# A held-over retention, a fourth raw buffer and longer paces in a hybrid attention/retention step

## The chip, the cores and the metric

The kernel runs on one core of a Trainium2 chip. The metric is the device time of one execution in microseconds (us), taken as the median of several executions. A profile is one more execution, recorded by the hardware; it has a time of its own.

The engines are named as in the profile: PE does the matmuls (PEld loads the stationary operand), DVE and ACT do elementwise work, POOL does masks and issues some DMAs, SP issues most DMAs. An engine works through its instructions in order. An instruction whose input isn't there yet holds up whatever stands behind it on the same engine or DMA queue.

## The reference

One step of a one-layer encoder over a prompt of 1024 frames and 8 running streams of 16 frames (128 sample frames), model width 2048, all in float32:

```
h = rms_norm(x, norm_pre);  p = h @ w_in            # 2048 x 8192
q_sb,k_sb,v_sb,gate_sb, q_r,k_r,v_r,gate_r = split(p)   # 8 heads of 128 each
stick-breaking: z = q k^T / sqrt(128); a = exp(log_sigmoid(z) + sum of later log_sigmoid(-z)), strictly causal; o = a v
retention (rotary q, k; chunks of 64): o = (q k^T * decay) v + decay_read * q S;  S = gamma^n S + k^T (decay_write v)
y = concat(head_rms_norm(o) * silu(gate));  out = y @ w_out;  x = x + rms_norm(out, norm_post)
```

The sample frames use a cache of 1024 past keys and values and a retention state per stream. The new keys, values and states are outputs too.

## The kernel before

**Tiles and groups.** Tokens come in tiles of 128 rows. Group 0 (`gi` 0) is prompt tiles 0 to 3 and the sample tile, group 1 (`gi` 1) is prompt tiles 4 to 7. For each group a loop runs over 8 heads, and for each head over "panels" of projection matmuls: `rows` (values and gates, 192 matmuls in group 1, L467), `ret_keys` and `ret_queries` (48 matmuls each, L410), `attention` (48 for the queries and 48 for the keys). A product of two float32 operands is made of three matmuls, so each weight block is split into a high and a low half by ACT and DVE (L173, L174). The order of the panels is rows, ret_keys, ret_queries, attention; in the last head of group 1 it is rows, attention, ret_keys, ret_last.

**Jobs and ticks.** All other work is in generators, called jobs: `ret_branch` (retention of one head, L1068 on), `sb_branch` (stick-breaking attention, L1094 on, with `stick_breaking` L781), `decode` (sample attention over the cache), and loads and splits for the output projection. A job yields a number of ticks; the panels call `tick()` after each product matmul (0.75 tick each in `rows`), and a tick runs at most one step of a job that is due. So a "pace" such as `D_RET` is a count of product matmuls to be put between two steps. `drain(job)` calls `tick()` until a job is done, with no matmul of a panel between: whatever is due in those ticks, of any job, is written out back to back.

**The planner.** The written order is a priority and not the final order. Tile's planner lays out each engine's order by simulating the engines: it takes the first instruction in the written order whose inputs are there by its own costs. Once laid out, the order is fixed, and on the chip an engine waits where the costs were too low.

**Around the changed places.** A head's retention builds `rk` and `rq` with rotary (`rope`, L507), writes `rk` to memory and reads it back in pieces to transpose it (`turn_out` L692, `turn_in` L701, DVE L797/L772/L1083), then does four blocks: scores (L957), output (L975, L982), state (L992, L997), one `D_RET` between output and state and another before the next block. `finish` normalises, gates, turns the output around through memory and stores it in `s_y`. In `sb_branch` each tile has matmuls z (L807), sigmoids, a scan (L737), a product (L738), a turn through memory (POOL L692, L701), a transpose (L797) and the product with the values (L834). `D_TB` stands between z and the rest, `D_TR` ahead of the last two products with the values. For group 0 the attention output is transposed into `kT`, a tile with one buffer.

For head 0 of group 1, `ret_keys` drains the retention of head 7 of group 0 ahead of its own `rope`. `attention` then drains the attention and the decode jobs of that head too and swaps the buffers `ip` and `psd` for `ip2` and `psx`.

The output projection is seven products of quarter matrices. In the last head, `first_left` (L1127) prepares the left operand of the first: `left` (L333) loads four pairs of blocks in three raw buffers `mr` (the fourth load waits until the first pair is split) and splits them. Its steps are taken between the weight blocks of the panel `ret_last`. Then come the products (5,0), (5,1), (1,0), (3,0), (3,1), under which the last retention and attention run: 72, 72, 72, 48 and 48 matmuls, one tick per matmul.

Of the kernel before, what the change touches and what calls it, by code (L numbers as in the profile page):

```python
# [18 lines left out]
P = 128  # L19
D = 2048  # L20
KT = D // P
H = 8
# [44 lines left out]
MR = 3  # L67
# [26 lines left out]
def tile_hybrid_step(  # L94
# [238 lines left out]
    def left(gi, n, hi, lo, bufs, tag, deep, wait):  # L333
        src = LEFT[n]
        raw = []

        def load(pair):
            r = bufs.tile([P, 2, 256], F32, name=tag, tag=tag, bufs=deep)
            if src[0] == "y":
                rows = s_y[gi][src[1] * H // 2 + pair][:, :, src[2] * 256 : src[2] * 256 + 256]  # L340
            else:
                rows = s_s[gi][pair][:, :, src[1], :]
            pin(nc.sync.dma_start(r, rows))
            raw.extend((r[:, 0], r[:, 1]))

        for pair in range(deep):
            load(pair)
        yield wait
        for h in range(HT):
            pin(*split(hi[h], lo[h], raw.pop(0)))  # L350
            if h % 2 and h // 2 + deep < HT // 2:
                load(h // 2 + deep)
            yield D_OP
# [127 lines left out]
    with ExitStack() as s1:  # L481
# [299 lines left out]
        def stick_breaking(g, h, out, q2, k2, rest):  # L781
# [3 lines left out]
            for step in range(len(todo) + lag):  # L785
# [33 lines left out]
                if step < len(todo):  # L819
                    if early:  # L820
                        yield D_TB[phase[0]]
# [3 lines left out]
                if step >= lag:  # L825
# [4 lines left out]
                    if step >= len(todo) and (early or step > len(todo)):  # L830
                        yield D_TR[phase[0]] + overlap()
# [10 lines left out]
        waiting = []  # L842

# [108 lines left out]

        def retention(gi, g, h, out, rq, rk, rkn, rv, dT, natural):
# [14 lines left out]
            for i in range(4):  # L968
# [3 lines left out]
                elif SAMPLE in g["tiles"]:  # L972
                    nxt = scores(4, 1)
                po = acc_tile()
# [15 lines left out]
                yield D_RET[phase[0]]  # L990
# [11 lines left out]
                yield D_RET[phase[0]]  # L1002
# [4 lines left out]
        def sample_retention(h, out, sc, rq, rkn, rv):  # L1007
# [26 lines left out]
            if not read:  # L1034
                waiting.clear()
                read_states()
            po = read[0]
# [55 lines left out]

        def sb_branch(gi, g, h, out, q2, k2, kT, rest):  # L1094
# [18 lines left out]
        summed, sampled, lefts, mine = [], [], [], {}  # L1113

# [12 lines left out]
        def first_left():  # L1127
# [3 lines left out]
            return left(0, 5, *mine[0, 5], wp, "mr", MR, D_LEFT)  # L1131
# [3 lines left out]
        for gi, g in enumerate(GROUPS):  # L1135
# [6 lines left out]
            for h in range(H):  # L1142
# [11 lines left out]
                def ret_queries(acc=None):  # L1154
                    rows_in["rq"] = rope(acc or project(g, mov, col(4, h)), "rq", *ropes)

                def ret_keys(acc=None):
# [4 lines left out]
                    acc = acc or project(g, mov, col(5, h))  # L1162
                    drain(ret_job)
                    ret_job = Job(ret_branch(gi, g, h, rows_in, rope(acc, "rk", *ropes)), D_NAT[phase[0]])
# [13 lines left out]
                def attention():  # L1178
# [9 lines left out]
                    if gi == 1 and h == 0:  # L1188
                        drain(sub)
                        late.close()  # L1190
# [473 lines left out]
```

## Time and profile before

| | |
|---|---|
| time, median of 3 runs | 2242.17 us (2240.48 to 2243.14) |
| the profiled execution | 2244.6 us, span of its instructions 2242.4 us |
| PE busy / share of the span | 2218.3 us / 99% |
| DVE, ACT, POOL busy | 1264.3, 919.3, 430.5 us |
| mean DMA rate | 209 GB/s |
| granted TensorE clock | 0.999 |

PE is busy for nearly the whole span, so a change can only take away idle time of PE, or add to it. The records of matmuls overlap, since a matmul's end is modelled: two starts of a full product are closer together than one record is long, and a stall shows as idle time only beyond that overlap. In the timelines a row gives start, duration, engine, line, operation, tiles, shape and count; in brackets at its end stand the idle time of the engine ahead of it and what ended it.

### The profile page before, as it was taken

What the parts mean: (1) busy time and instruction counts of PE and PEld (TensorE: products, weight loads), DVE (VectorE), ACT (ScalarE), POOL (GpSimd) and SP (SyncE); (2) the same over time, 40 slices, a digit from 0 to 9 for tenths busy, and PEclk for the clock granted to TensorE, in tenths of its full rate; (3) what the DMA queues carried; (4) which work ended last, traced back from release to release, by engine and by line L of the source; (5) the groups of instructions that cost most, each with busy time, mean ns of one, the idle gap of its engine ahead of it and who ended that gap; (6) DMA issues with size and microseconds to landing.
All of it is one profiled execution on the core that took longest, in us unless ns stands there. A gap on an engine that the chain in (4) does not pass through costs nothing. (4 is left out here: it accounts for less than half of the span.)

```text
span 2242.4 us, 34745 instructions
## 1 busy us (share of the span) xinstructions
PE 2218.3 (99%) x12046; PEld 1886.3 (84%) x12046; DVE 1264.3 (56%) x2690; ACT 919.3 (41%) x1999; POOL 430.5 (19%) x723
## 2 busy tenths in 40 slices
PE   9999999999999999999999999999999999999998
PEld 8888889798888979888788888888888887778887
DVE  5435445453454545356666665756666657556577
ACT  7423333333333333334433443443434445545463
POOL 1022131222213132221222112120202212000020
PEclk9999999999999999999999999999999999999999
DMA  8567575566757656677868777878788777865785
GB/s 294 178 197 204 172 198 174 176 190 209 193 173 196 183 171 194 202 202 269 233 182 239 220 227 232 235 228 235 221 233 230 211 224 188 235 220 161 220 224 170
DMA packets 379297, 467.83 MB, mean 209 GB/s; under 512 B 118128, under 2 KB 235632, under 8 KB 378608
## 3 DMA queue, kind: packets, MB, share of 16 engines
q1 hardware_dynamic: 250608, 290.58, 43.8%
q0 software_dynamic: 36432, 95.72, 15.8%
q10 hardware_dynamic: 92080, 79.32, 11.2%
q8 instruction: 94, 1.54, 0.3%
q14 instruction: 83, 0.68, 0.1%
HBM read 364.56 MB, written 106.95 MB: 210 GB/s over the span
## 5 line engine op out<-in xcount | busy, mean ns | idle before, releaser
L467 PE MATMUL accm<-whn,mh 128*128 128x512 f32 x1152 | 452.1, 393 | 0.5 <-DVE rq L513 0.5
L467 PE MATMUL accm<-whn,ml 128*128 128x512 f32 x1152 | 452.3, 393 | 0.0
L467 PE MATMUL accm<-wln,mh 128*128 128x512 f32 x1152 | 451.3, 392 | 0.0
L410 PE MATMUL acc<-ml,wh 128*128 128x256 f32 (+2 forms) x1536 | 445.8, 341 | 0.6 <-DVE ml L180 0.3
L173 ACT ACTIVATE wh<-wr 128x512 fp32r<-128x512 f32 x408 | 255.9, 631 | 459.6 <-PE acc L410 190.0
L410 PE MATMUL acc<-mh,wl 128*128 128x256 f32 (+2 forms) x1536 | 444.1, 340 | 0.0
L410 PE MATMUL acc<-mh,wh 128*128 128x256 f32 (+2 forms) x1536 | 442.2, 339 | 0.5 <-ACT mh L179 0.4
L174 DVE TENSOR_TENSOR wl<-wr,wh 128x512 fp32r<-128x512 f32 x408 | 279.4, 688 | 261.5 <-ACT wh L173 241.7
L174 DVE TENSOR_TENSOR wln<-wrn,whn 128x512 fp32r<-128x512 f32 x256 | 175.9, 689 | 285.7 <-ACT whn L173 282.8
L173 ACT ACTIVATE whn<-wrn 128x512 fp32r<-128x512 f32 x256 | 161.4, 631 | 391.7 <-PE accm L467 259.3
L410 PEld LDWEIGHTS acc<-mh,wl 128*128 128x128 f32 x1536 | 281.2, 188 | 23.8 <-issue 5.4
L410 PEld LDWEIGHTS acc<-mh,wh 128*128 128x128 f32 x1536 | 283.0, 188 | 20.3 <-ACT mh L179 0.9
L410 PEld LDWEIGHTS acc<-ml,wh 128*128 128x128 f32 x1536 | 280.3, 188 | 20.9 <-DVE ml L180 1.6
L467 PEld LDWEIGHTS accm<-whn,mh 128*128 128x128 f32 x1152 | 216.5, 188 | 44.6 <-DVE rq L513 0.9
L467 PEld LDWEIGHTS accm<-whn,ml 128*128 128x128 f32 x1152 | 216.5, 188 | 43.4 <-issue 0.8
L467 PEld LDWEIGHTS accm<-wln,mh 128*128 128x128 f32 x1152 | 216.5, 188 | 43.1
L701 POOL DMA_DIRECT2D be<-s_be x128 | 94.2, 742 | 159.2 <-DMA s_be<-be 132.3
L737 DVE TENSOR_TENSOR_SCAN kp<-kp 128x1152 f32<-128x1152 f32 (+4 forms) x40 | 82.7, 2069 | 56.1 <-POOL kp L726 28.3
L1262 PE MATMUL a<-wh,mh 128*128 128x512 f32 x240 | 94.6, 394 | 0.1
L1265 PE MATMUL a<-wl,mh 128*128 128x512 f32 x240 | 93.9, 391 | 0.3 <-DVE wl L174 0.3
L1266 PE MATMUL a<-wh,ml 128*128 128x512 f32 x240 | 93.5, 390 | 0.0
L726 POOL TENSOR_SCALAR_AFFINE_SELECT kp<-kp 128x128 f32<-128x128 f32 x40 | 13.6, 341 | 362.9 <-ACT kp L720 362.8
(287 smaller groups left out, 3011.9 us busy)
## 6 DMA issues: line engine op xcount, KB each, us to landing
wrn<-w_rows SPq DMA_DIRECT2D x256, 256.0 KB, 3.7
wr<-w_cols SPq DMA_DIRECT2D x255, 256.0 KB, 4.4
kcT<-cache_k POOLq DMA_DIRECT2D x64, 512.0 KB, 4.7
vc<-cache_v SPq DMA_DIRECT2D x64, 512.0 KB, 5.2
wr<-s_b SPq DMA_DIRECT2D x80, 256.0 KB, 3.7
wr<-w_out SPq DMA_DIRECT2D x80, 256.0 KB, 4.1
br<-w_out SPq DMA_DIRECT2D x64, 256.0 KB, 4.6
s_b<-br ACTq DMA_DIRECT2D x32, 512.0 KB, 4.6
```

The source lines that it names most:

```text
L173: nc.scalar.activation(hi, src, AF.Copy),
L174: nc.vector.tensor_tensor(lo, src, hi.bitcast(F32), ALU.subtract),
L410: last = nc.tensor.matmul(a[:, :m], lhs[:, j, :], rhs[w][:, j, o : o + m], start=(w == 0 and j == 0 and n == 0), stop=(w == KT // WQ - 1 a ...
L467: anchor[0] = nc.tensor.matmul(banks[t], lhs[q][:, j, ts], rhs, start=(k == 0 and n == 0), stop=(k == KT - 1 and n == 2),)
L701: q.dma_start(raw[32 * i : 32 * i + 32, :].rearrange("p (k a) -> p k a", a=32), s[:, :, 32 * i : 32 * i + 32].rearrange("k (j b) a -> b (k ...
L726: nc.gpsimd.affine_select(blk, blk, pattern=[[-1, P]], base=0, channel_multiplier=1, compare_op=ALU.is_gt, fill=fill,)
L737: nc.vector.tensor_tensor_scan(rev, rev, rev, 1.0, ALU.mult, ALU.bypass)
L1262: ins = nc.tensor.matmul(a, hi[k][:, ts], wh, start=first, stop=False)
L1265: nc.tensor.matmul(a, hi[k][:, ts], wl, start=False, stop=False)
L1266: anchor[0] = nc.tensor.matmul(a, lo[k][:, ts], wh, start=False, stop=last)
```

## The change

- **Retention held over.** In head 0 of group 1, `ret_keys` no longer drains the retention of head 7 of group 0. It ticks only until the last read of `rk` has been written out (`until`), makes its own `rk`, and starts its own retention job behind the old one (`behind` asks every 3 ticks). `ret_queries` does likewise for `rq`. The old job is drained in `attention`, after the drain of `sub`.
- **A fourth raw buffer.** In the last head a tile `gg` (the gates of head 6, no longer used) serves `left` as a fourth raw buffer. The fourth pair is loaded after the panel `ret_keys` and no longer in `ret_last`.
- **Longer paces.** For the last head of group 1 alone, `at_last` adds 6 ticks to `D_TB` (4 times), 12 to `D_TR` (2 times) and 4 to `D_RET` (8 times).

```diff
--- before.py
+++ after.py
@@ -330,12 +330,12 @@
             r = nxt
             yield pace[2]
 
-    def left(gi, n, hi, lo, bufs, tag, deep, wait):
+    def left(gi, n, hi, lo, bufs, tag, deep, wait, spare=None):
         src = LEFT[n]
         raw = []
 
-        def load(pair):
-            r = bufs.tile([P, 2, 256], F32, name=tag, tag=tag, bufs=deep)
+        def load(pair, r=None):
+            r = bufs.tile([P, 2, 256], F32, name=tag, tag=tag, bufs=deep) if r is None else r
             if src[0] == "y":
                 rows = s_y[gi][src[1] * H // 2 + pair][:, :, src[2] * 256 : src[2] * 256 + 256]
             else:
@@ -346,9 +346,14 @@
         for pair in range(deep):
             load(pair)
         yield wait
+        ahead = deep
+        if spare is not None:
+            load(deep, spare.pop().rearrange("p t j d -> p (t j d)")[:, :512].rearrange("p (i n) -> p i n", i=2))
+            ahead += 1
+            yield 0
         for h in range(HT):
             pin(*split(hi[h], lo[h], raw.pop(0)))
-            if h % 2 and h // 2 + deep < HT // 2:
+            if h % 2 and h // 2 + deep >= ahead and h // 2 + deep < HT // 2:
                 load(h // 2 + deep)
             yield D_OP
 
@@ -818,7 +823,7 @@
                     yield D_TB[phase[0]] + overlap()
                 if step < len(todo):
                     if early:
-                        yield D_TB[phase[0]]
+                        yield D_TB[phase[0]] + at_last(phase[0], h, 6)
                     be = be[:, :n]
                     turned = turn_out(be.rearrange("p (k c) -> p k c", c=P), f"s_be{h}_{t}", nc.gpsimd)
                     rows.append((kp, be, turned))
@@ -828,7 +833,7 @@
                     n = (t + 1) * P
                     at = kp[:, :n].rearrange("p (k q) -> p k q", q=P)
                     if step >= len(todo) and (early or step > len(todo)):
-                        yield D_TR[phase[0]] + overlap()
+                        yield D_TR[phase[0]] + overlap() + at_last(phase[0], h, 12)
                     po = acc_tile()
                     for j in range(t + 1):
                         nc.tensor.matmul(po[:, :P], at[:, j, :], rest["vn"][j], start=(j == 0), stop=(j == t))
@@ -840,6 +845,9 @@
             return rows
 
         waiting = []
+
+        def at_last(gi, h, more):
+            return more if (gi, h) == (1, H - 1) else 0
 
         def with_scores():
             while waiting:
@@ -950,6 +958,12 @@
             oT = op.tile([P, P], F32, name="doT", tag="doT", bufs=1)
             Job(out.finish(0, 0, h, 4, oT, y_of(0, h)[:, 4 * P : 5 * P]))
 
+        spent = set()
+
+        def until(what):
+            while what not in spent:
+                tick()
+
         def retention(gi, g, h, out, rq, rk, rkn, rv, dT, natural):
             def scores(i, kind):
                 bs = slice(i * P, (i + 1) * P)
@@ -971,6 +985,7 @@
                     nxt = scores(i + 1, 0)
                 elif SAMPLE in g["tiles"]:
                     nxt = scores(4, 1)
+                    spent.add(("rk", h))
                 po = acc_tile()
                 nc.tensor.matmul(po[:, :P], sc, rv[:, i, :], start=True, stop=True)
                 if i == 0:
@@ -987,7 +1002,7 @@
                         od, po[:, P : 2 * P], dec[:, h, 0:1], od, ALU.mult, ALU.add
                     )
                 out.done(i)
-                yield D_RET[phase[0]]
+                yield D_RET[phase[0]] + at_last(gi, h, 4)
                 pS = score_tile("pS")
                 nc.tensor.matmul(pS[:, :P], rkn[:, i, :], rv[:, i, :], start=True, stop=True)
                 Sn = op.tile([P, P], F32, name="S", tag="S", bufs=3)
@@ -999,7 +1014,7 @@
                     )
                 S = Sn
                 sc = nxt
-                yield D_RET[phase[0]]
+                yield D_RET[phase[0]] + at_last(gi, h, 4)
             nc.scalar.dma_start(s_S[h] if gi == 0 else s_prompt[0, 0, h], S)
             if SAMPLE in g["tiles"]:
                 yield from sample_retention(h, out, sc, rq, rkn, rv)
@@ -1034,6 +1049,7 @@
             if not read:
                 waiting.clear()
                 read_states()
+            spent.add(("rq", h))
             po = read[0]
             yield D_OFF
             od = out.o[:, i, :]
@@ -1091,6 +1107,11 @@
             yield from retention(gi, g, h, out, rows_in["rq"], rk, rkn, rv, dT, natural)
             yield from out.finish(1, gi, h, 0, rkn.rearrange("p k d -> p (k d)"), y_of(gi, H + h))
 
+        def behind(job, steps):
+            while not job.done:
+                yield 3
+            yield from steps
+
         def sb_branch(gi, g, h, out, q2, k2, kT, rest):
             tiles, nt = g["tiles"], len(g["tiles"])
             off = 0 if gi == 0 else 4
@@ -1111,6 +1132,7 @@
             return x_cols[:, KT * o + k * n : KT * o + (k + 1) * n]
 
         summed, sampled, lefts, mine = [], [], [], {}
+        held_over, spare = [], []
 
         def kept(i):
             return [[half[i][:, h // 2, h % 2 * 256 : h % 2 * 256 + 256] for h in range(HT)] for half in mov]
@@ -1128,7 +1150,7 @@
             while stored[0] < HT + H:
                 tick()
             mine[0, 5] = kept(0)
-            return left(0, 5, *mine[0, 5], wp, "mr", MR, D_LEFT)
+            return left(0, 5, *mine[0, 5], wp, "mr", MR, D_LEFT, spare)
 
         ret_job = sb_job = sub = loads = None
         after = [[], []]
@@ -1152,7 +1174,10 @@
                         rooted_tables(ropes, g["pieces"])
 
                 def ret_queries(acc=None):
-                    rows_in["rq"] = rope(acc or project(g, mov, col(4, h)), "rq", *ropes)
+                    acc = acc or project(g, mov, col(4, h))
+                    if (gi, h) == (1, 0):
+                        until(("rq", H - 1))
+                    rows_in["rq"] = rope(acc, "rq", *ropes)
 
                 def ret_keys(acc=None):
                     nonlocal ret_job
@@ -1160,7 +1185,16 @@
                         lefts.append(first_left())
                         next(lefts[0])
                     acc = acc or project(g, mov, col(5, h))
+                    if (gi, h) == (1, 0):
+                        held_over.append(ret_job)
+                        until(("rk", H - 1))
+                        steps = ret_branch(gi, g, h, rows_in, rope(acc, "rk", *ropes))
+                        ret_job = Job(behind(ret_job, steps), D_NAT[phase[0]])
+                        return
                     drain(ret_job)
+                    if (gi, h) == (1, H - 1):
+                        spare.append(ep.tile([P, 5, 2, P], F32, name="gg", tag="gg", bufs=2))
+                        next(lefts[0])
                     ret_job = Job(ret_branch(gi, g, h, rows_in, rope(acc, "rk", *ropes)), D_NAT[phase[0]])
 
                 def ret_last():
@@ -1187,6 +1221,7 @@
                     drain(sb_job)
                     if gi == 1 and h == 0:
                         drain(sub)
+                        drain(held_over[0])
                         late.close()
                         banks.append(s1.enter_context(tc.tile_pool(name="psx", bufs=1, space=PSUM)))
                         ip = s1.enter_context(tc.tile_pool(name="ip2", bufs=1))
```

## The prediction

> **What bounds the kernel now.** I read the engines' busy time first, then stretches of PE alone, then what PE waited for.
>
> ```profile
> span 2242.4 us, 34745 instructions
> PE 2218.3 (99%) x12046; PEld 1886.3 (84%) x12046; DVE 1264.3 (56%) x2690; ACT 919.3 (41%) x1999; POOL 430.5 (19%) x723
> ```
>
> PE is idle for 2242.4 - 2218.3 = 24.1 us. No edit here removes a matmul, so what can be won lies in those 24.1 us and in a short overlap at each stall. The stretches say where they are (columns: stretch, length, PE busy, instructions, clock, DMA share, GB/s):
>
> ```profile
> 0.00:20.00 20.00, 17.82 (x116) 1.00 0.86 286
> 1088.00:1150.00 62.00, 59.25 (x342) 1.00 0.72 193
> 1150.00:1760.00 610.00, 608.97 (x2932) 1.00 0.79 227
> 1863.00:1945.00 82.00, 76.86 (x374) 1.00 0.78 202
> 2225.00:2242.40 17.40, 8.26 (x60) 0.86 0.65 186
> ```
>
> Start and end (2.2 and 9.1 us) are untouched. The change works in 1088 to 1150 (head 0 of group 1, 2.75 us idle) and 1863 to 1945 (the last head under the first output products, 5.14 us). 610 us of ordinary heads lose 1.03 us: that is the normal rate. PE's waits have names:
>
> ```profile
> PE pa L834 <- DVE kp L797: 2.7, 4, 1.8
> PE pd L936 <- DMA vc<-cache_v: 2.6, 2, 1.6
> PE rs L957 <- DVE rq L515: 2.5, 4, 2.0
> PE pa L982 <- DVE S L997: 0.9, 2, 0.4
> ```
>
> Every one of these lines belongs to a job that an edit touches. One price first: two free-running products start 0.23 us apart but each record is 0.39 long, so a stall costs its idle time plus 0.16 us.
>
> ```profile
> 1150.04 0.39 PE L467 MATMUL accm<-whn,mh 128*128 128x512 f32 x1
> 1150.26 0.39 PE L467 MATMUL accm<-wln,mh 128*128 128x512 f32 x1
> ```
>
> **The retention held over, what it removes.** When `ret_keys` of head 0 ends, the old retention has just read its states and still has paces of 3+3+3+9+32+36 ticks ahead, so the drain runs 90 ticks without a product. In them the decode job writes out both of its sets of value products, whose pace of 36 ticks (`D_VC`) should have covered the second set's loads:
>
> ```profile
> 1106.58 2.80 PE L936 MATMUL pd<-vc,kp 128*32 128x256 f32 x48
> 1112.21 0.64 PE L936 MATMUL pd<-vc,kp 128*32 128x256 f32 x8 [1.03 <-DMA vc<-cache_v]
> 1115.54 0.64 PE L936 MATMUL pd<-vc,kp 128*32 128x256 f32 x8 [1.57 <-DMA vc<-cache_v]
> 1127.66 0.49 PE L957 MATMUL rs<-rq,rk 128*128 128x128 f32 x2
> 1107.28 1.53 SPq L902 DMA_DIRECT2D vc<-cache_v  x2
> ```
>
> The two loads of 1107.28 are waited for until 1112.21 and 1115.54, up to 1115.5 - 1107.7 = 7.8 us. Without the drain 36 ticks are 36 products of 0.23, or 8.2 us: covered, narrowly. Gain 1.03 + 1.57 + 2 x 0.16 = 2.9. The scores of the new head (1127.66) are one of L957's four waits for `rq`, 2.5 us in all, of which the longest is 2.0; the other three are 0.17 each. They now come some 90 ticks later: gain 0.17 + 0.16 = 0.3. Together **3.2** (from 0 if the loads are slower among the weights, to 3.2).
>
> **What it adds.** `until` finds both reads already written out and costs no tick. The old job has three panels of 48 ticks, 144, for its 90; the drain behind `sub` is empty. But the clock loses 90 ticks, and the attention of group 0's head 7 needs 19+9+14+25+9+20+9+32+36 = 173 from the end of `ret_keys`: 29 too many. Its last step, transpose into `kT` and scaling, is now drained at the end of the keys' panel (call it T), where before it was long done:
>
> ```profile
> 1116.11 1.16 PE L834 MATMUL pa<-vv,kb 128*128 128x128 f32 x8
> 1122.32 0.37 ACTq L692 DMA_DIRECT2D s_o<-so  x1
> 1127.73 2.80 POOL L701 DMA_DIRECT2D so<-s_o  x4 [1.15 <-DVE rq L515]
> 1134.52 0.70 DVE L772 STREAM_TRANSPOSE kT<-so 128x512 f32<-128x512 f32 x1
> 1136.76 0.48 DVE L773 TENSOR_SCALAR so<-kT,pre 128x512 f32<-128x512 f32 x1
> 1150.39 0.68 DVE L486 TENSOR_TENSOR kT<-acc,roots 128x512 f32<-128x512 f32 x1
> ```
>
> From that product with the values to a free `kT` went 1137.24 - 1116.11 = 21.1 us. Its turn moves to 96 ticks after `ret_keys`, 48 products (10.9 us) ahead of T, so `kT` is free near T + 10.2. The new keys can't leave their PSUM bank before, where now they do at T + 0.35 (1150.39 against 1150.04). `rows` of head 1 has four row tiles in four banks, and one is this bank. Three of the four can go on for the four weight blocks that the buffers hold (36 products, 8.2 us), and the new retention's matmuls are due there as well. If the planner lays it out so, the loss is 0; if it trusts the turn to be quick and PE stops after the first two row tiles (6 products, 1.4 us), it is 10.2 + 0.7 - 1.4 = 9.5. A turn that comes later than planned is in the trace already:
>
> ```profile
> 1939.17 0.71 DVE L772 STREAM_TRANSPOSE be<-so 128x512 f32<-128x512 f32 x1 [3.13 <-DMA so<-s_o]
> 1940.23 0.49 PE L1262 MATMUL a<-wh,mh 128*128 128x512 f32 x1
> 1941.06 0.50 PE L1265 MATMUL a<-wl,mh 128*128 128x512 f32 x1 [0.34 <-DVE wl L174]
> ```
>
> DVE stood 3.13 us with weight splits queued behind it, and PE lost 0.83 - 0.23 = 0.6 at one place and 0.3 just ahead (its starts go from 0.23 to 0.54 apart). The case is of the same kind, so I take **-0.9** (0 to -9.5).
>
> **The fourth raw buffer.** In `ret_last` the fourth load of `left` waits for the first buffer's split, and the splits of its pair stand ahead of the rotary copies on ACT:
>
> ```profile
> 1856.36 0.53 SPq L343 DMA_DIRECT2D mr<-s_s  x1
> 1863.47 0.72 ACT L173 ACTIVATE mh<-mr 128x256 fp32r<-128x256 f32 x2 [4.29 <-DMA mr<-s_s]
> 1865.26 0.60 ACT L511 ACTIVATE sw<-acc 64x512 f32<-64x512 f32 x1
> 1869.19 0.69 DVE L515 TENSOR_TENSOR rq<-rq,sw 128x512 f32<-128x512 f32 x1
> 1869.93 0.49 PE L957 MATMUL rs<-rq,rk 128*128 128x128 f32 x2 [1.97 <-DVE rq L515]
> ```
>
> 7.1 us pass from issue to split, ACT idles 4.29, and PE waits 1.97 for `rq`. The tile `gg` is free (both its readers are drained), so the load goes out ahead of the first weight block's 12 products, 2.7 us earlier or more, and at least as much of ACT's 4.29 goes: more than PE's 1.97. DVE's 0.95 us product L738 and the weight splits behind the same wait come earlier too. Gain 1.97 + 0.16 = **2.1** (0 to 2.1). The page "DMA: Bandwidth & Descriptors" of the Trainium skill, section "Anatomy of one DMA", gives a DMA 2.0 us plus its bytes over 436 GB/s; for this 256 KB pair that makes an estimate of 2.6 us. By that rule the pair would have been there before ACT asked and this edit would be worth nothing, a sum of 3.1 in place of 5.2. The trace disagrees, with 7.1 us in a queue that weights share.
>
> **The longer paces.** Three stalls lie in their reach:
>
> ```profile
> 1877.87 2.02 DVE L737 TENSOR_TENSOR_SCAN kp<-kp 128x896 f32<-128x896 f32 x1
> 1880.12 0.49 PE L982 MATMUL pa<-S,rq 128*128 128x128 f32 x2 [0.45 <-DVE S L997]
> 1900.47 0.71 PE L834 MATMUL pa<-vo,kp 128*128 128x128 f32 x4 [0.43 <-DVE kp L797]
> 1912.41 0.78 POOL L701 DMA_DIRECT2D be<-s_be  x1 [5.60 <-issue]
> 1921.20 1.16 PE L834 MATMUL pa<-vo,kp 128*128 128x128 f32 x8 [1.81 <-DVE kp L797]
> ```
>
> `D_RET` goes from 5 to 9 products per step (1.1 to 2.0 us), enough for a state update that stands behind a 2.02 us scan: **0.6** (0.45 + 0.16). For the product with the values of tile 6, turn and input are close: its turn, counted in yields, is product 93 of this stage, and it moves by 24 + 12 ticks, past its input; **0.6** (0.43 + 0.16). Tile 7 is another matter. Its turn is about product 117, and PE did it after 184:
>
> ```profile
> L1262 PE MATMUL a<-wh,mh 128*128 128x512 f32 x62 | 25.2, 406 | 0.0
> L1265 PE MATMUL a<-wl,mh 128*128 128x512 f32 x61 | 24.1, 395 | 0.0
> L1266 PE MATMUL a<-wh,ml 128*128 128x512 f32 x61 | 23.9, 391 | 0.0
> ```
>
> (62 + 61 + 61 from 1863.1 to 1919.1.) The planner already held it back until the transposed tile should be there, and was wrong by 1.8 us, with POOL's last piece of the read-back 5.60 us late. The paces add 48 ticks to its turn and 18 to its z, so the turn (165) stays ahead of the place its input sets (202). The wait can recur as it is; of 2.0 I count **0.3** (0 to 2.0). The jobs end 32 and 48 ticks later, 7 and 11 us. The attention's results are then stored about 100 products before the next stage reads them, so nothing downstream is late. The stall of 1940 moves along and stays. The steps of both jobs now share more of DVE and ACT with the splits of the next left operands; for new waits in 144 us of re-laid order I take **-0.7**, above the 1.03 of 610 us because these jobs lost 5 us here (0 to -2).
>
> **Sum.** 3.2 - 0.9 + 2.1 + 0.6 + 0.6 + 0.3 - 0.7 = 5.2. The profiled execution, 2244.6 with a span of 2242.4, becomes 2239.4. It lay 2.4 above the median of the runs, 2242.17, so the median becomes **2237.0**.
>
> **Rivals.**
> - *The waits only move.* The planner's places follow inputs, not paces: the three pace terms are 0, new waits take the full 2, and the turn into `kT` costs 3.1 as DVE's wait did. 3.2 - 3.1 + 2.1 - 2 = 0.2, so 2242.0. For it: tile 7 stands 67 products behind its turn. Against: the retention's steps are at their turn.
> - *All of it.* Nothing lost at `kT`, no new waits, tile 7 cured: 3.2 + 2.1 + 0.6 + 0.6 + 2.0 = 8.5, so 2233.7. For it: 610 us of ordinary heads lose 1.03.
> - *The bank at T.* PE stops for `kT` for the whole 9.5 us: 3.2 - 9.5 + 2.1 + 1.5 - 0.7 = -3.4, so 2245.6. It decides the sign from 6.1 us on. For it: POOL can add 5.60 us that no planner sees. Against: 8.2 us of other rows are at hand.
> - *The buffer isn't the cause.* The pair is slow because the queue is full, and an earlier load only delays the weights: 5.2 - 2.1 = 3.1, so 2239.1.
>
> **How the numbers follow.** Chances: forecast 0.47, waits only move 0.21, all of it 0.16, bank 0.09, buffer 0.07. The forecast's own range is 2234.5 to 2240. The overall range 2232 to 2243.5 takes in the second and third cases and leaves out most of the bank's. 0.2% is 4.5 us, about what a measurement of this kernel can tell; faster means under 2237.7. That is 0.7 of the forecast (0.33) and all of "all of it" (0.16): 0.49. Slower means over 2246.7: nearly half of the bank's case and a little for what I haven't seen: 0.06. The rest is 0.45.
>
> **What would show it.** The L936 products should no longer wait for `vc`; `rs` at the start of the output products should follow its neighbours without idle time; L982 and the tile 6 product likewise; the tile 7 product should still wait. PE between the end of the keys' panel of head 0 and the z products of that head should show at most 1 us idle, and the old head's L772 should stand there with a DVE wait for its read-back. The prediction is wrong if PE idles there for several us, if L936 still waits, or if idle time of over 2 us turns up under new names between 1863 and 1945.

## The result, and the profile after

The changed kernel takes 2238.32 us (median of 17 runs, 2236.62 to 2240.49), the kernel before 2241.77 (17 runs, 2240.03 to 2245.82). The ratio is 0.9982, 95% interval 0.9975 to 0.9989: 2.5 to 5.6 us, 3.45 by the medians. It is faster, by a little less than the 0.2% that the prediction named as its bound. The profiled execution took 2237.49 us.

The page's head, for the changed kernel (lines of the code move by 5 to 35: L834 is now L839, L936 L944, L957 L971, L982 L997, L737 L742, L738 L743, L797 L802, L692 L697, L701 L706, L772 L777, L486 L491, L1262/1265/1266 L1297/1300/1301):

```profile
span 2235.5 us, 34741 instructions
PE 2217.4 (99%) x12046; PEld 1887.0 (84%) x12046; DVE 1264.5 (57%) x2690; ACT 919.7 (41%) x1999; POOL 431.9 (19%) x723
```

PE's busy time fell by 0.9 us and its idle time from 24.1 to 18.1. The stretches of PE alone (stretch, length, PE busy, instructions, clock, DMA share, GB/s):

```profile
1088.00:1150.00 62.00, 62.00 (x359) 1.00 0.72 201
1863.00:1945.00 82.00, 79.19 (x384) 1.00 0.78 210
```

Head 0 of group 1 lost 2.75 us and now loses nothing; the last head lost 5.14 and loses 2.81. Three of PE's waits over the whole kernel (total, times, longest):

```profile
PE pa L839 <- DVE kp L802: 2.4, 3, 1.9
PE a L1297 <- ACT mh L1357: 0.8, 1, 0.8
PE rs L971 <- DVE rq L520: 0.6, 3, 0.2
```

In the last head 1.9 of the first and the 0.8 are left. The waits for `vc` and for the retention's state are gone from the list, and of those for `rq` the 2.0 us one; the three of 0.2 stand in other heads. The single instructions that answer to the rows quoted before:

```profile
1107.06 1.93 PE L944 MATMUL pd<-vc,kp 128*32 128x256 f32 x32
1117.78 1.93 PE L944 MATMUL pd<-vc,kp 128*32 128x256 f32 x32
...
1863.65 0.49 PE L971 MATMUL rs<-rq,rk 128*128 128x128 f32 x2
...
1897.76 1.05 PE L839 MATMUL pa<-vo,kp 128*128 128x128 f32 x8
...
1904.43 0.50 PE L1297 MATMUL a<-wh,mh 128*128 128x512 f32 x1 [0.79 <-ACT mh L1357]
1915.49 1.16 PE L839 MATMUL pa<-vo,kp 128*128 128x128 f32 x8 [1.86 <-DVE kp L802]
```

The two sets of cached value products now stand 10.7 us apart, which covers their loads. The scores at the start of the output products and the product of tile 6 come without a wait. Tile 7 (1915.49) waits as before, and one wait is new: the fourth matmul of the third output product (1,0) stands behind ACT's collecting of an earlier sum (1904.43).

One thing did not fit: the medians are 3.45 us apart, the two profiled spans 6.9.

### The profile page after: what moved, and what is told of

It reads as the page before. It is cut to its first block, busy times and chain, and to the rows that moved or that the text cites. A ratio compares the mean times of both kernels' runs of the same rounds, so it can differ in the third digit from the quotient of the medians.

```text
span 2235.5 us, 34741 instructions
## 1 busy us (share of the span) xinstructions
PE 2217.4 (99%) x12046; PEld 1887.0 (84%) x12046; DVE 1264.5 (57%) x2690; ACT 919.7 (41%) x1999; POOL 431.9 (19%) x723
## 5 line engine op out<-in xcount | busy, mean ns | idle before, releaser
L706 POOL DMA_DIRECT2D be<-s_be x128 | 94.4, 743 | 158.3 <-DMA s_be<-be 135.1
L742 DVE TENSOR_TENSOR_SCAN kp<-kp 128x1152 f32<-128x1152 f32 (+4 forms) x40 | 82.6, 2065 | 52.3 <-POOL kp L737 27.9
L1297 PE MATMUL a<-wh,mh 128*128 128x512 f32 x240 | 94.7, 395 | 0.8 <-ACT mh L1357 0.8
L706 POOL DMA_DIRECT2D kb<-s_be x128 | 76.8, 607 | 27.1 <-DMA s_be<-kb 23.8
```

Source lines behind the costliest of these rows:

```text
L706: q.dma_start(raw[32 * i : 32 * i + 32, :].rearrange("p (k a) -> p k a", a=32), s[:, :, 32 * i : 32 * i + 32].rearrange("k (j b) a -> b (k ...
L742: nc.vector.tensor_tensor_scan(rev, rev, rev, 1.0, ALU.mult, ALU.bypass)
L1297: ins = nc.tensor.matmul(a, hi[k][:, ts], wh, start=first, stop=False)
```

## The experiments

All kernels were run several times beside the kernel before on the same chip. "Against before" is the difference of medians; in brackets the 95% interval of the ratio.

| run | what it has | median, us (runs) | against before, us (ratio) |
|---|---|---|---|
| e1_held | held-over retention alone | 2239.50 (11) | -2.65 (0.9980 to 0.9997) |
| e2_spare | fourth raw buffer alone | 2241.85 (11) | -0.30 (0.9990 to 1.0008) |
| e3_paces | longer paces alone | 2241.52 (11) | -0.63 (0.9989 to 1.0007) |
| e4_before_again | the kernel before | 2241.84 (11) | -0.31 (0.9990 to 1.0008) |
| e5_after_again | the changed kernel | 2238.59 (11) | -3.44 (0.9975 to 0.9992) |
| e6_tile7 | changed, tile 7's product later | 2239.12 (11) | -2.91 (0.9981 to 0.9999) |
| e7_kT | changed, `kT` free at once | 2238.25 (11) | -3.78 (0.9976 to 0.9993) |
| e8_ret_pace | changed, only the retention's pace | 2235.76 (7) | -6.27 (0.9961 to 0.9982) |
| e9_ret_pace_again | the same | 2235.40 (6) | -6.63 (0.9956 to 0.9980) |
| e10_no_pace | held over + buffer, no longer pace | 2238.04 (11) | -3.99 (0.9973 to 0.9990) |
| e11_tr_pace | changed without the 6 ticks | 2234.90 (6) | -7.13 (0.9959 to 0.9982) |
| e12_tb_pace | changed without the 12 ticks | 2238.20 (11) | -3.83 (0.9972 to 0.9990) |

The first four ran on one chip, the next four on a second, the last four on a third. Where two kernels are compared below with "+-", it is the difference of their means with a 95% interval worked out from the runs of the two.

**The same kernel twice.** e4 and e5 have no edit. They were run for a second trace.

> The kernel before, unchanged, as a second trace. By the timed runs nothing differs: 0 us. Its profiled run lay 2.4 to 2.8 us above the median of its runs, and the two profiled spans (before, after) are 6.9 us apart where the medians are 3.45 apart. Theory A: some of the stalls shown there (1.03 and 1.57 for vc, 1.97 for rq, 1.81 at tile 7) vary from run to run and were at the long end, so this trace has 1 to 3 us less idle time at those places. Theory B: the stalls are the same to 0.2 us, and the 2.8 us lie elsewhere, in the start and the end of the kernel or in PE's own busy time.

The page and the waits of the kernel before, second trace, and two of its single rows:

```profile
span 2238.7 us, 34745 instructions
...
PE pa L834 <- DVE kp L797: 1.8, 3, 1.2
PE pd L936 <- DMA vc<-cache_v: 1.7, 2, 1.1
...
PE rs L957 <- DVE rq L515: 1.5, 4, 0.9
PE a L1265 <- DVE wl L174: 1.0, 2, 0.9
...
1112.77 0.64 PE L936 MATMUL pd<-vc,kp 128*32 128x256 f32 x8 [1.07 <-DMA vc<-cache_v]
1115.17 0.64 PE L936 MATMUL pd<-vc,kp 128*32 128x256 f32 x8 [0.63 <-DMA vc<-cache_v]
```

The order of the instructions is the same, and so are nearly all the places at which PE waits (0.30 us at 1433, 0.34 at 1941 and one of the two waits of 0.45 for the retention's state don't come back). The lengths aren't: 1.70 us for `vc` where the first trace had 2.60, 1.5 for `rq` where it had 2.5 (the long one 0.88 for 1.97), 1.8 at the products with the values for 2.7, 1.0 for weight splits in the output products (L1265) for 1.6. These four make 3.4 of the 3.7 us between the two spans. Theory A holds: the profiled execution on which the prediction was made was long, and mostly at stalls that the change addresses. The second one is short in its turn: at 2240.85 us it lies 1.0 under the median of its runs, so a usual execution lies between the two.

> The changed kernel, unchanged, as a second trace and as the yardstick of the other runs of this call: 3.45 us faster than the kernel before (2.5 to 5.6). Theory A (stalls vary from run to run): the waits left in its trace, 1.86 us at tile 7's product with the values and 0.79 at the sum of the output products, come back with other lengths, and the idle time of 2.81 us between 1863 and 1945 differs by 0.5 us or more. Theory B: they come back the same to 0.2 us.

The second trace of the changed kernel has a span of 2234.6 us, 0.9 less than the first; tile 7's wait is 0.5 in place of 1.86, the new one at the collected sum 0.6:

```profile
PE a L1297 <- ACT mh L1357: 0.6, 1, 0.6
```

Theory A again. The two traced executions of the changed kernel are also among its quickest (2237.49 of 2236.62 to 2240.49, and 2236.67, the lowest of its 11), and the first of the kernel before among its slowest; that is where the 6.9 us came from. A single trace shows places well and sizes only to about a microsecond per stall (1.09 us apart at `rq`, 1.40 at tile 7).

**The held-over retention alone.** The edit is the change's part in `ret_queries` and `ret_keys`, `until`, `behind` and the late drain; `at_last` gives 0 and no `spare` is filled.

```diff
-            return more if (gi, h) == (1, H - 1) else 0
+            return 0
...
-            return left(0, 5, *mine[0, 5], wp, "mr", MR, D_LEFT, spare)
+            return left(0, 5, *mine[0, 5], wp, "mr", MR, D_LEFT)
...
-                        spare.append(ep.tile([P, 5, 2, P], F32, name="gg", tag="gg", bufs=2))
-                        next(lefts[0])
+                        pass
```

> The kernel before with the held-over retention alone; no fourth raw buffer, no longer paces. The prediction's terms for it are 3.2 us won (2.9 at the value products that wait for vc, 0.3 at the scores that wait for rq) and 0 to 0.9 given back at the bank of the new keys: 2.3 to 3.2 us faster. The trace of the changed kernel has PE with no idle time at all between 1088 and 1150, so the theory now takes the upper end: about 3 us faster, no wait for vc, none at kT, and the stalls of the last head (1.97 for rq, 0.45 at the state, 0.43 and 1.81 at the products with the values) as in the kernel before. Rival, the waits only move: 0 to 1 us faster, with new idle time of 2 us or more between 1088 and 1160.

It was 2.65 us faster by the medians (2.1 +- 1.0 by the means). PE in the stretch of head 0, in the kernel before (second trace) and here:

```profile
1088.00:1150.00 62.00, 60.15 (x347) 1.00 0.72 197
```

```profile
1088.00:1150.00 62.00, 62.00 (x358) 1.00 0.72 201
```

The 1.85 us of idle time are gone and nothing came in their place. By the medians this part is most of the change's gain.

**The bank at T.** In the changed kernel the old head's output passes through `kT` after the panel of the new keys has ended, and the new keys wait for it. e7 takes the shared tile away: the old head's output goes through a part of `rows`.

```diff
-            yield from out.finish(0, gi, h, 0, rows[2][1] if gi else kT, y_of(gi, h)[:, :NB_TOK])
+            yield from out.finish(0, gi, h, 0, rows[2][1] if gi else rows[3][1] if h == H - 1 else kT, y_of(gi, h)[:, :NB_TOK])
```

> The changed kernel, but the output of group 0's last head is transposed into another tile than kT (a part of rows), so that the new keys can leave their PSUM bank at once and not 7.6 us after the panel's end. Theory: the planner fills that gap with other products, PE has no idle time there either way, so 0 us against the changed kernel (within 0.5), with the copy into kT back at less than 1 us after the end of the panel. Rival, the late bank costs the 0.9 us of the prediction in waits further on: 0.9 us faster than the changed kernel.

The changed kernel, DVE and POOL around T = 1142.83 (the first `accm` product of head 1's rows; the panel of the keys has ended there):

```profile
1141.14 2.60 POOL L706 DMA_DIRECT2D so<-s_o  x4 [11.43 <-DVE wln L174]
1149.02 0.70 DVE L777 STREAM_TRANSPOSE kT<-so 128x512 f32<-128x512 f32 x1
1150.47 0.69 DVE L491 TENSOR_TENSOR kT<-acc,roots 128x512 f32<-128x512 f32 x1
```

The same with the tile taken away:

```profile
1142.98 0.69 DVE L491 TENSOR_TENSOR kT<-acc,roots 128x512 f32<-128x512 f32 x1
1149.13 0.71 DVE L777 STREAM_TRANSPOSE kb<-so 128x512 f32<-128x512 f32 x1
```

The new keys leave their bank 7.5 us earlier (1142.98 against 1150.47), and the time is the same: 2238.25 against 2238.59, +0.4 +- 1.3 by the means. PE worked through both. As a cost the late bank is nothing that can be measured, and the theory holds.

**The fourth raw buffer alone.** Of the change, only the tile `gg` as a fourth buffer in `left`, and the step that loads it:

```diff
+                    if (gi, h) == (1, H - 1):
+                        spare.append(ep.tile([P, 5, 2, P], F32, name="gg", tag="gg", bufs=2))
+                        next(lefts[0])
```

> The kernel before with the fourth raw buffer alone. Theory: the 1.97 us wait for rq at the scores of the last head goes, and with it ACT's 4.29 us for mr, so 2.1 us faster; the waits for vc (1.03 and 1.57) and the stalls of tiles 6 and 7 stay. Rival, the buffer isn't the cause (the queue is full, so an earlier load only makes another one late): 0 us, ACT waits about as long for gg or for the next mr, and PE's wait for rq stays over 1 us. Second rival: the wait goes but the jobs behind it run into the stalls of tiles 6 and 7 earlier, which grow by as much: 0 to 1 us.

It was 0.30 us faster by the medians, 0.1 +- 0.8 by the means: neither 2.1 nor clearly nothing. The traces say why. First the kernel before (second trace), then this one:

```profile
1854.95 0.53 SPq L343 DMA_DIRECT2D mr<-s_s  x1
...
1860.98 0.72 ACT L173 ACTIVATE mh<-mr 128x256 fp32r<-128x256 f32 x2 [3.20 <-DMA mr<-s_s]
...
1861.75 0.39 PE L1262 MATMUL a<-wh,mh 128*128 128x512 f32 x1
...
1862.77 0.60 ACT L511 ACTIVATE sw<-acc 64x512 f32<-64x512 f32 x1
...
1867.45 0.49 PE L957 MATMUL rs<-rq,rk 128*128 128x128 f32 x2 [0.88 <-DVE rq L515]
```

```profile
1857.99 0.74 ACT L173 ACTIVATE mh<-gg 128x256 fp32r<-128x256 f32 x2
...
1862.09 0.39 PE L1288 MATMUL a<-wh,mh 128*128 128x512 f32 x1
...
1862.76 0.60 ACT L516 ACTIVATE sw<-acc 64x512 f32<-64x512 f32 x1
...
1867.27 0.49 PE L971 MATMUL rs<-rq,rk 128*128 128x128 f32 x2 [0.36 <-DVE rq L520]
```

The edit does what it says: the splits come 3.0 us earlier and without a wait. But the rotary copy behind them stands where it stood. It also waits for the panel's last product, which is the one just ahead of the first output product; with the buffer the copy follows that output product by 0.67 us, without it by 1.02 here and by 2.11 in the first trace (1865.26 after 1863.15). So the buffer can win 1.44 us in the long execution and 0.35 in the other, not the whole wait: what is left (0.36) is the chain from the panel's end to `rq`. On top of the held-over retention it shows no wait at all at these scores in e10, where e1 had 1.01. The buffer isn't needed for that in every execution: in e3's trace, which has no fourth buffer, the load lands early enough (5.4 us from its issue to the split), the copy follows the first output product by 0.68 us and the scores wait 0.38.

**The paces.** e3 has the longer paces without the other two parts: its diff against the kernel before is the change's, without `until`, `behind`, `held_over` and `spare`. e8 to e12 are the changed kernel with one or more of three edits. e8 and e9 have the first and the second, e11 the first, e12 the second, e10 all three:

```diff
-                        yield D_TB[phase[0]] + at_last(phase[0], h, 6)
+                        yield D_TB[phase[0]]
```

```diff
-                        yield D_TR[phase[0]] + overlap() + at_last(phase[0], h, 12)
+                        yield D_TR[phase[0]] + overlap()
```

```diff
-                yield D_RET[phase[0]] + at_last(gi, h, 4)
+                yield D_RET[phase[0]]
...
-                yield D_RET[phase[0]] + at_last(gi, h, 4)
+                yield D_RET[phase[0]]
```

e6 is the changed kernel with tile 7's turn later:

```diff
-                        yield D_TR[phase[0]] + overlap() + at_last(phase[0], h, 12)
+                        yield D_TR[phase[0]] + overlap() + at_last(phase[0], h, 12 if step == len(todo) else 72)
```

> The kernel before with the longer paces of the last head alone. The prediction's terms: 0.6 for the state of the retention, 0.6 for tile 6, 0.3 for tile 7, less 0.7 for new waits: 0.8 us faster (0.2 to 1.5), with the wait of tile 7's product with the values still at 1.5 us or more. Rival, the paces cure tile 7 too: 3.2 us faster. Rival, places follow inputs: within 0.5 us of the kernel before, with the 0.45 and 0.43 us waits still there.

0.63 us faster by the medians, 0.4 +- 1.4 by the means. The waits at the retention's state and at tile 6 are gone from the last head, tile 7's is 1.2, and 0.9 has come at the collected sum. That is in line with the 0.8 of the prediction, and too small to tell it from 0.

> The changed kernel with 60 more products of pace ahead of tile 7's product with the values in the last head (72 in place of 12), so that its turn stands behind the place that its transposed input set. Theory: the 1.86 us wait there goes, 1.9 us faster than the changed kernel, about 5.3 faster than the kernel before. Rival 1, the wait is POOL's late read-back and moves with it, or DVE's stall behind it only shows at another product: the same as the changed kernel to 0.5 us. Rival 2: the later end of the job makes the next stage wait for the stored rows: slower than the changed kernel by 1 us or more.

In the order of the instructions the product of tile 7 moves from behind 186 output products to behind 225, and it no longer waits. It gains nothing: 2239.12 against 2238.59, 1.1 +- 1.3 slower by the means. In its trace idle time stands behind it, at weight splits:

```profile
1922.59 1.06 PE L839 MATMUL pa<-vo,kp 128*128 128x128 f32 x8
...
1941.43 0.51 PE L1297 MATMUL a<-wh,mh 128*128 128x512 f32 x1 [0.54 <-ACT wh L173]
1942.15 0.50 PE L1300 MATMUL a<-wl,mh 128*128 128x512 f32 x1 [0.22 <-DVE wl L174]
```

With one more of 0.22 that is 0.98 us, where the trace of e5 on the same chip had 0.46 at tile 7 and 0.23 at a split. This is nearest to rival 1, that a wait is taken from one place and shows at the next; rival 2, slower by 1 us or more, isn't excluded by 1.1 +- 1.3.

> The changed kernel with only the retention's longer pace kept; the attention's paces of the last head are those of before. Theory: the wait at tile 6's product with the values (0.43 in the trace of before) returns, so 0.6 us slower than the changed kernel; tile 7's wait stays at about 1.9, and the 0.79 us wait at the sum of the output products goes or moves, since it belongs to the relaid order. Rival: with the order of the rest as it now is (rq earlier by 2 us) no wait returns, and the paces of the attention are worth nothing: within 0.3 us of the changed kernel, or faster.

The theory fell. The rival had it right that the attention's two paces are worth nothing, but not that they cost this much: without them the kernel is 2.6 +- 1.2 us faster than the changed kernel on the same chip. The next four runs took the paces apart.

> The kernel of the last run unchanged (fourth raw buffer, held-over retention, the retention's longer pace, the attention's paces of before), since its median came out 2.8 us under that of the changed kernel with few runs, and its own trace had a stall of 1.25 us in an ordinary head (at 1430 us) that no other trace of this form has. Theory: the gain is real; 5.5 to 6.5 us faster than the kernel before, tile 7's product with the values after 172 output products again without a wait, and the stall at 1430 gone from the trace. Rival: a lucky chip or few runs; 3.5 us, as the changed kernel.

> Held-over retention and fourth raw buffer, and every pace of the last head as before. In its instruction order tile 7's product stands after 184 output products, as in the kernel before. Theory, the retention's longer pace is what moves tile 7's chain forward: the parts add up to 2.65 + 0.3 = 2.9 us faster than the kernel before, with waits of about 0.45 at the state and 0.5 to 1.9 at tile 7. Rival, any longer pace costs time here: as fast as the kernel of the run before this, 6 us.

> The changed kernel without the 6 ticks ahead of the attention's next scores; the 12 ahead of the products with the values and the retention's longer pace are kept. Its order has tile 7's product after 172 output products, as with the retention's pace alone. Theory, the 6 ticks are what costs: 5.5 to 6.5 us faster than the kernel before and no wait at tile 7. Rival, the 12 ticks cost as well or alone: 3.5 to 4.5 us.

> The changed kernel without the 12 ticks ahead of the products with the values; the 6 ticks ahead of the next scores and the retention's longer pace are kept. Its order has tile 7's product after 186 output products, as the changed kernel. Theory, the 6 ticks are what costs: 3.5 us faster than the kernel before, the scan of tile 7 some 31 us after the first output product, and a wait of 0.5 to 1.9 us at tile 7. Rival, the 12 ticks cost: 5.5 us or more.

The gain repeats on another chip (e9: 6.63 us under the kernel before), so the first theory holds there. The stall at 1430 us isn't gone, as that theory had it: 1.10 us in e8's trace, 0.45 in e9's. The order of PE there is the same in e10, in e11 and in the changed kernel, whose traces show no idle time at that product, so what brings it stays open. Held over and buffer without any pace (e10) give 3.99, more than the parts' 2.9 but within their uncertainty. The retention's pace on top of it gives 2.6 +- 1.0 (e9 against e10). The 12 ticks change nothing that can be seen (e11 against e9: 0.06 +- 1.2 between the means). The 6 ticks take it all back: e11 is 2.8 +- 1.2 under e12, which has the 6 and not the 12, and e12 and e10 can't be told apart (0.2 +- 0.9).

What moves most is the chain of tile 7: mask on POOL, scan and product (L743) on DVE, write-out and read-back on POOL, transposition on DVE, product on PE. First e10, without the longer pace (the first read-back is tile 6's):

```profile
1880.48 3.01 POOL L706 DMA_DIRECT2D be<-s_be  x4 [3.39 <-DMA s_be<-be]
1883.50 0.31 POOL L731 TENSOR_SCALAR_AFFINE_SELECT kp<-kp 128x128 f32<-128x128 f32 x1
...
1890.02 2.28 DVE L742 TENSOR_TENSOR_SCAN kp<-kp 128x1024 f32<-128x1024 f32 x1
...
1894.42 0.90 POOL L697 DMA_DIRECT2D s_be<-be  x1 [10.38 <-DVE be L743]
1898.94 2.35 POOL L706 DMA_DIRECT2D be<-s_be  x3 [3.62 <-DMA s_be<-be]
1906.92 0.78 POOL L706 DMA_DIRECT2D be<-s_be  x1 [5.63 <-issue]
...
1914.17 1.25 DVE L802 STREAM_TRANSPOSE kp<-be 128x1024 f32<-128x1024 f32 x1 [0.34 <-issue]
...
1915.47 1.16 PE L839 MATMUL pa<-vo,kp 128*128 128x128 f32 x8 [0.75 <-DVE kp L802]
```

Then e9, with the retention's pace alone:

```profile
1878.34 0.68 POOL L731 TENSOR_SCALAR_AFFINE_SELECT kp<-kp 128x128 f32<-128x128 f32 x1
1879.05 2.36 DVE L742 TENSOR_TENSOR_SCAN kp<-kp 128x1024 f32<-128x1024 f32 x1 [0.19 <-POOL kp L731]
...
1881.68 3.01 POOL L706 DMA_DIRECT2D be<-s_be  x4 [2.42 <-DMA s_be<-be]
...
1886.25 0.90 POOL L697 DMA_DIRECT2D s_be<-be  x1 [1.56 <-issue]
1894.68 2.35 POOL L706 DMA_DIRECT2D be<-s_be  x3 [7.54 <-DMA s_be<-be]
1898.21 0.79 POOL L706 DMA_DIRECT2D be<-s_be  x1 [1.17 <-issue]
...
1908.34 1.24 DVE L802 STREAM_TRANSPOSE kp<-be 128x1024 f32<-128x1024 f32 x1
...
1911.00 1.06 PE L839 MATMUL pa<-vo,kp 128*128 128x128 f32 x8
```

The first output product starts at 1860.00 and 1860.17 in these two, so the times can be set side by side. In e9 POOL masks tile 7 ahead of tile 6's read-back; the scan waits for that mask, and fits on DVE between a state update (1878.01) and the next scores (1883.04). In e10 the mask stands behind the read-back on POOL, so the scan can't start before 1883.8; it comes at 1890.02, 11 us later than in e9, when the retention is over. The mask stands ahead of the read-back in e8 and e11 too, and behind it in every other kernel of the table: of these runs only those have it early that keep the longer pace of the retention and leave out the attention's 6 ticks. Why the planner turns the two around is not shown. The write-out, the last piece of the read-back and the transposition follow 8.2, 8.7 and 5.8 us earlier, and the product stands after 172 output products, 1.4 us behind its transposed tile, where in e10 it stood after 184 and waited for it. In the changed kernel the 6 ticks put the scan back:

```profile
1890.08 2.28 DVE L742 TENSOR_TENSOR_SCAN kp<-kp 128x1024 f32<-128x1024 f32 x1
```

That is 31.1 us behind its first output product (1858.97), as in e10 (30.0) and in e12 (31.2), against 18.9 in e9. PE's stretch from 1863 to 1945 in e9 and in e11:

```profile
1863.00:1945.00 82.00, 81.35 (x399) 1.00 0.77 217
```

```profile
1863.00:1945.00 82.00, 81.06 (x397) 1.00 0.75 215
```

0.65 and 0.94 us of idle time, where the changed kernel has 2.81 and 1.5 in its two traces, e10 1.89 and e12 2.28. By pairs that differ in one pace, e10 less e9 is 1.2 us and e12 less e11 1.3. Idle time leaves out what the overlap of the records hides, so the stage is better counted whole. Its 312 output products, with the 96 other matmuls among them, take from the start of the first output product to that of the 313th 84.4 us in e9 (1860.17 to 1944.56) and 84.7 in e11, 86.8 in e10 (1860.00 to 1946.79) and 87.8 in e12. The pairs are 2.4 and 3.1 us apart, about as much as the times (2.6 and 2.8), so the difference lies in this stage. The changed kernel takes 87.7 and 86.8 there, e8 86.2 in the trace of its slowest execution.

It is not all at tile 7. e10 idles 0.45 us at the retention's state, 0.43 at tile 6 and 0.75 at tile 7. e12 idles 0.9 at weight splits, only 0.16 at tile 7, where 0.5 to 1.9 was expected, and most at tile 6:

```profile
1898.26 1.16 PE L839 MATMUL pa<-vo,kp 128*128 128x128 f32 x8 [1.16 <-DVE kp L802]
```

e9 and e11 have none of these waits, and one of 0.59 that e10 and e12 lack, at an output of the retention (L990). The three kernels with the early chain are the three quick ones in the table; by way of which of these waits a pace costs its time is not shown.

**A version that beats both** is among these runs: the change without the 6 ticks (e11), 2234.90 us, ratio 0.9970 (0.9959 to 0.9982) to the kernel before, and some 3.5 us under the changed kernel, each measured against the kernel before. e8 and e9 can't be told from it.

## Why the prediction was right or wrong

It gave 2237.0 us from a sum of 5.2; the median came out at 2238.32, a gain of 3.45 (2.5 to 5.6). The forecast's case held in kind. That the total came so near is partly luck, since the terms miss in both directions:

- *Held-over retention, +3.2, and -0.9 at `kT`.* The mechanism held in each step: no wait for `vc`, no idle time at the scores, and PE fed through T by the other row tiles and the new retention. Alone it gave 2.65 (2.1 +- 1.0) against 2.3 predicted. Inside that, the -0.9 was 0 (e7), the case that the prediction named "if the planner lays it out so", and the 2.9 was too much for the usual execution: the second trace has 1.70 of waits for `vc`, so 2.0 with the overlaps. The 0.3 at the new head's scores has the right size by a wrong reading: they are none of L957's four waits, of which the short three stand at 1228, 1330 and 1636 and are in the changed kernel too; what was lost there is a start 0.53 us behind the product ahead (1127.13 to 1127.66) in place of 0.23. One sign failed: L777 was to stand with a DVE wait for its read-back and shows none.
- *Fourth raw buffer, +2.1.* The term was mis-sized, alone 0.3 (0.1 +- 0.8). The step that failed is "at least as much of ACT's 4.29 goes: more than PE's 1.97". It compared the length of a wait that goes with the one behind it, and left out the second thing that the rotary copies wait for, the panel's last product, which left 1.44 us to be won in that trace, 0.35 in the next and nothing in e3's. The estimate of 2.6 us rests on a fit that the Trainium skill, "DMA: Bandwidth & Descriptors", section "Anatomy of one DMA", gives for DMAs issued by GpSimd, while SP issues this pair. From issue to split the pair took 6.0 us in the second trace and 5.4 in e3's, so the traces disagree with that estimate again; the edit was worth little all the same, for a reason that lies behind the load.
- *`D_RET`, +0.6.* Right in sign and too small. With the rest of the change and without the attention's paces it is 2.6 +- 1.0. The prediction priced the one wait that it saw at L982 (0.45 in e10, none in e9). What it didn't see is that with this pace, and without the attention's 6 ticks, the planner lays tile 7's mask 5 us and its scan 11 us earlier.
- *Tile 6, +0.6, and tile 7, +0.3.* Tile 6's wait went and tile 7's stayed, as predicted, and its place moved from 184 to 186 products, not to 202. The failed step is the one that costs the paces as later turns alone. The 6 ticks stand between one tile's weights and its write-out, ahead of the next tile's z; with them tile 7's scan comes 11 us later, and e11 against e12 puts the cost at -2.8 +- 1.2. The 12 ticks are worth nothing that can be seen.
- *New waits, -0.7.* The trace of the changed kernel has 0.79 at the collected sum, 0.59 in its second: the right size. e3 has 0.9 there, e1 and e10, without the longer paces, 0.3 and 0.2, so most of it comes with the paces.
- *The paces as a block* were to bring 0.8. With the other parts they bring -0.55 by the medians of e10 and the changed kernel (-0.6 +- 1.5 by the means, on two chips). The +2.6 and the -2.8 are not two prices to be added: both are the step between the two places of tile 7's chain, and no run has the retention's pace out and the 6 ticks in. Held-over retention and buffer together were to bring 4.4 and brought 3.99 (4.4 +- 1.1 by the means). So by the medians the 1.75 us between the predicted and the measured gain lie mostly in the paces, though not clear of the noise.
- *From the profiled execution to the median.* The prediction took 2.4 us off the result, and left the terms as read from an execution that was 2.4 us long. The second trace shows that most of what the first execution has over the second lay in those terms.

Of the rivals, "the waits only move" described the paces as a block rightly and not the sum, for the held-over retention's gain is real; "all of it" had the 0 at `kT` and missed tile 7; "the bank at T" is excluded by e7, "the buffer isn't the cause" was near in its price and wrong in its reason.

## What to carry to other kernels

Before a stall's full length is credited to an edit, list everything that the released instruction waits for: the gain ends at the second-latest. A pace in front of one step is a delay for every step behind it in the same job, and it can turn the planner's order around on an engine that is mostly idle (here POOL, 19% busy, where tile 7's mask came to stand ahead of tile 6's read-back or behind it). So try paces one at a time: here the same kind of edit gained 2.6 us between the retention's steps and cost 2.8 inside the attention's chain, which was late already. And where an edit is aimed at stalls of a microsecond, take a second trace of the unchanged kernel first.

## What the runs showed of the hardware that was not expected

The same program, with the same order of instructions, spread over 2238.9 to 2244.7 us in 33 runs on one chip, and of the 3.7 us between two traces of it 2.0 lie at two stalls with a DMA behind them: 0.63 us and 1.57 at the same load of `vc`, 0.88 and 1.97 behind the same load of `mr`. Whether one order spreads less than another can't be told from these runs: eleven runs of one kernel lie within 2.9 us in e2 and e12 and within 6.5 in e3.

POOL's four read-back pieces of 1024 columns are issued in 0.8 us each, but before the fourth POOL stood 5.63 us in e10 and 1.17 in e9, with 7.54 instead of 3.62 us waiting for the write-out ahead of the first three. The two waits are nearly the same together: from the end of the write-out to the issue of the fourth piece it is 11.6 us in e10 and 11.1 in e9 (9.8 in the changed kernel). What holds the fourth piece was not tried.
